# Convolution and max-pool on one core: the first quarter of the first pair loaded as fp32, identity and zeros set ahead of the casting loads, and all instructions in another order

## The chip, the cores and the metric

The kernel runs on one core of a Trainium2 chip. The metric is device time in microseconds (us), the median of several runs. A profile is of one execution; its span is the time from the first to the last instruction, and a little lies around it. The engines are PE (TensorE, matrix products; PEld is its weight load), DVE (VectorE), ACT (ScalarE), POOL (GpSimd) and SP (SyncE, which issues DMA transfers). ACT and POOL can issue transfers too; those of POOL can change the type on the way.

## The reference

Sixteen images of 64 channels and 64x64 points are convolved with a 3x3 kernel into 128 channels, with a border of zeros, and each 2x2 block of the result is reduced to its maximum.

```python
batch, c_in, h, w, c_out, k = 16, 64, 64, 64, 128, 3
x_pad = np.pad(x, ((0, 0), (0, 0), (1, 1), (1, 1)))
conv[b, co] += weight[co, ci, kh, kw] * x_pad[b, ci, kh:kh+h, kw:kw+w]      # over ci, kh, kw
output[b, c, i, j] = np.max(conv[b, c, 2*i:2*i+2, 2*j:2*j+2])
```

## The kernel before, in words

**Tiling.** Two images share the 128 partitions (64 channels each), so there are eight pairs, held as bf16 in `rows_x`. A pair is cut into four quarters of 16 rows. That gives 32 steps, numbered in the order of `SEQ`; `W01` is pair 0, quarter 1. In a step, each of the two images (lane 0 and 1) has two accumulators A and B of 128x512 fp32, one bank each of the eight banks of PSUM. A product with one lane uses 64 of PE's 128 rows, and the products of the two lanes run side by side.

**Two ways to make a step.** With g0, g1, g2 the weights of the three kernel rows and r(-1), r0, r1, r2 four input rows around a pair of output rows:

- Kind K (steps 0, 2, 6 and 7): A = (g2-g1) r1 + g0 r(-1) (products `PAa`, `PAb`), B = (g0-g1) r0 + g2 r2 (`PBa`, `PBb`), then B = max(A, B), then B += g1 (r0+r1) (`PR`). The weight blocks are called D2, G0, D0, G2, G1. D2 and D0 are differences; G0, G1 and G2 are plain copies of the weights.
- Kind W (all others): products with differences and sums of rows, `P2` (block GM, rows E = r0-r1), `P0` and `P3` (blocks G0, G2, rows V), `P1` (block GP, rows S = r0+r1). GM and GP need the sum g0+g2, `gsum`.

Each product has three taps, one matrix product per column shift of the kernel. For step 0 alone the products of kind K are cut into an upper half (`a`, pooled rows 0 to 3) and a lower half (`b`).

**What the engines do for a step.** DVE and POOL make the row sums and differences (tokens `KS`, `S`, `E`, `V`, and `S2`, `E2`, `V2` for two steps at once, line 219). ACT copies A out (`EV`, lines 401 and 403) and, in kind W, seeds B from A (`SE`, line 415). DVE takes the maximum of B and that copy (`MX`, line 427). At the end the columns are reduced: ACT copies the odd ones out (`OD`, line 431) and DVE takes the maximum (`CM`, line 448), or DVE reduces alone (`RM`, line 436). Then SP stores the result.

**The start.** SP loads the weights (`wraw`) and the first nine rows of the first pair as fp32 (`first`, line 184). POOL loads all other rows with a cast to bf16 (`load`, line 180); the ranges stand in `LOADS`, and the first three are issued before anything else (`EARLY = 3`). Then POOL makes the identity for the transposes, while DVE sets `zeros` and the border rows of `rows_x` to zero. PE multiplies ones by ones until the weights are there. DVE and ACT make the weight blocks in bf16 (tokens `c.`, lines 211, 212 and 219), PE transposes each (`T`, line 252, three products), and DVE or ACT copies it out of PSUM into `wt` (`TV`, lines 263 and 267). `XO` and `XE` cast the odd and the even rows of `first` into `rows_x`.

**What sets the order.** Nothing is scheduled by a compiler. `ORDER` is a list of tokens; each emits one instruction (a product token one tap) on the engine that it names, and each engine works through its own instructions in that order. An instruction waits for what it reads and for the buffer that it writes, and everything behind it on its engine waits too. Two rules beside it: a row operation on POOL is put behind the last one on DVE (`behind`), and a transfer takes one of eight semaphores in turn.

## Time and profile before

| | us |
|---|---|
| median of the runs (99.55 to 99.73) | 99.69 |
| the profiled execution | 99.57 |
| its span | 97.8 |
| PE busy (845 products) | 92.4 |
| DVE busy | 88.9 |
| ACT busy | 82.9 |
| POOL busy | 68.4 |
| first product of step 0 starts at | 5.55 |
| last load from HBM issued by POOL, time to landing (median of the 1 MB loads) | 13.5 |

Times in a timeline count from the span's start. A row of a timeline has the start, the time taken, the engine, the line, the operation, the tile written and read and the number of instructions merged; in brackets stands the idle time before it and what ended that. Instructions of an engine overlap a little, so two of 0.35 us in a row can take 0.62. A row of the DMA view has a queue, the packets, the megabytes and the share of the time of the 16 DMA engines; a row of an issue ends with the time from issue to landing. The granted clock of PE was 1.00 in nearly all of the span.

### The profile page before, as it was taken

To read this page: it belongs to the slowest core of one execution; us is meant where nothing else is said; L and a number is where in the kernel's file an instruction comes from. 1 tells how busy PE (TensorE), PEld (TensorE's weight loads), DVE (VectorE), ACT (ScalarE), POOL (GpSimd) and SP (SyncE) were. 2 spreads that over 40 slices of the span, in tenths; PEclk is the share of its full clock that TensorE was granted. 3 is DMA by queue.
4 is the path that set the end of the run, shared out by engine and by line. 5 is a ranking of instruction groups with operands and counts; after the bars stand their busy time and mean duration, and the time that the engine had idled before them with its cause. 6 is when DMAs were issued, how large, how long until landed. Compare 5 with 4: busy or idle time off the path is not lost.

```text
span 97.8 us, 2315 instructions
## 1 busy us (share of the span) xinstructions
PE 92.4 (94%) x845; PEld 57.6 (59%) x845; DVE 88.9 (91%) x172; ACT 82.9 (85%) x177; POOL 68.4 (70%) x60
## 2 busy tenths in 40 slices
PE   6998999999999999999999999999999999999920
PEld 2394554555886885666667555564555557777600
DVE  3459999999999999999999999999998999997960
ACT  5466688599779999999999999999989999889830
POOL 5994545936488867989584876759499779599200
PEclk9999999999999999999999999999999999999998
DMA  2999999999999999999999740405050503254052
GB/s 55 237 145 196 169 204 216 218 233 230 250 225 244 225 245 330 238 227 299 225 230 291 285 144 27 188 3 189 32 214 0 217 4 137 84 214 144 17 188 80
DMA packets 7675, 17.36 MB, mean 178 GB/s; under 512 B 624, under 2 KB 2544, under 8 KB 7024
## 3 DMA queue, kind: packets, MB, share of 16 engines
q0 software_dynamic: 2160, 8.24, 43.3%
q1 hardware_dynamic: 5216, 8.72, 25.6%
q10 hardware_dynamic: 288, 0.26, 0.8%
q8 instruction: 6, 0.10, 0.4%
q14 instruction: 5, 0.04, 0.1%
HBM read 17.07 MB, written 8.39 MB: 260 GB/s over the span
## 4 chain that ended last, share of the span: by engine, by line
PE 83%; POOL 5%; DVE 4%; issue 3%; ACT 1%; ACTq 0%; POOLq 0%
PE acc L369 82%; POOL rows_x L180 4%; DVE o L448 2%; DVE acc L427 1%; POOL gsum L219 1%; ACT acc L415 1%; PE acc L252 1%; DVE wq L219 1%; ACT ev L401 1%; POOL ident masks.py:199 0%; POOL ident masks.py:197 0%; ACTq L415 0%; POOLq L534 0%
## 5 line engine op out<-in xcount | busy, mean ns | idle before, releaser
L369 PEld LDWEIGHTS <-wt 64*128 64x128 bf16 x816 | 55.2, 94 | 31.2 <-issue 1.8
L369 PE MATMUL acc<-wv,wt 64*128 64x504 bf16 (+1 forms) x264 | 49.9, 377 | 0.0
L427 DVE TENSOR_TENSOR acc<-acc,ev 128x512 f32<-128x512 f32 x64 | 42.7, 689 | 1.2 <-ACT acc L415 0.5
L369 PE MATMUL acc<-ws,wt 64*128 64x512 bf16 (+1 forms) x168 | 40.8, 376 | 0.0
L369 PE MATMUL acc<-we,wt 64*128 64x512 bf16 (+1 forms) x168 | 39.3, 377 | 0.0
L401 ACT ACTIVATE ev<-acc 128x512 f32<-128x512 f32 x56 | 32.7, 605 | 1.8 <-PE acc L369 1.7
L415 ACT COPY acc<-acc 128x512 f32<-128x512 f32 x56 | 32.2, 590 | 2.1 <-PE acc L369 1.3
L219 POOL TENSOR_TENSOR ws<-rows_x 128x512 bf16<-128x512 bf16 (+1 forms) x12 | 17.6, 1477 | 4.2 <-DVE wv L219 1.9
L431 ACT COPY od<-acc 128x256 f32<-128x256 f32 x49 | 18.0, 379 | 2.8 <-PE acc L369 2.3
L219 POOL TENSOR_TENSOR we<-rows_x 128x512 bf16<-128x512 bf16 (+1 forms) x10 | 15.4, 1542 | 6.3 <-DVE wv L219 3.8
L448 DVE TENSOR_TENSOR o<-acc,od 128x256 f32<-128x256 f32 (+1 forms) x48 | 19.1, 420 | 0.1
L369 PE MATMUL acc<-rows_x,wt 64*128 64x504 bf16 (+7 forms) x120 | 16.5, 332 | 0.0
L219 POOL TENSOR_TENSOR wv<-rows_x 128x1024 bf16<-128x1024 bf16 (+1 forms) x6 | 14.7, 2449 | 2.3 <-DVE ws L219 1.6
L369 PE MATMUL acc<-vh,wt 64*128 64x504 bf16 (+1 forms) x72 | 16.0, 377 | 0.0
L219 POOL TENSOR_TENSOR vh<-rows_x 128x512 bf16<-128x512 bf16 x8 | 9.2, 1155 | 5.6 <-DVE we L219 3.1
L436 DVE TENSOR_REDUCE o<-acc 128x256 f32<-128x512 f32 x15 | 10.2, 680 | 0.0
L180 POOL DMA_DIRECT2D rows_x<-in_x_dram x15 | 8.6, 575 | 2.1 <-DMA rows_x<-in_x_dram 1.3
L219 DVE TENSOR_TENSOR wv<-rows_x 128x1024 bf16<-128x1024 bf16 (+1 forms) x11 | 9.8, 891 | 0.0
L369 PE MATMUL acc<-ks,wt 64*128 64x504 bf16 (+1 forms) x24 | 6.0, 376 | 0.0
L403 ACT COPY ev<-acc 128x512 f32<-128x512 f32 x8 | 4.5, 586 | 0.9 <-PE acc L369 0.9
L219 DVE TENSOR_TENSOR we<-rows_x 128x1024 bf16<-128x1024 bf16 (+1 forms) x9 | 5.1, 564 | 0.0
L219 DVE TENSOR_TENSOR ws<-rows_x 128x512 bf16<-128x512 bf16 (+1 forms) x8 | 4.7, 588 | 0.0
(26 smaller groups left out, 24.1 us busy)
## 6 DMA issues: line engine op xcount, KB each, us to landing
out_dram<-o SPq DMA_DIRECT2D x13, 512.0 KB, 6.5
rows_x<-in_x_dram POOLq DMA_DIRECT2D x5, 1024.0 KB, 13.5
rows_x<-in_x_dram POOLq DMA_DIRECT2D x4, 256.0 KB, 8.4
out_dram<-o SPq DMA_DIRECT2D x3, 256.0 KB, 2.9
rows_x<-in_x_dram POOLq DMA_DIRECT2D x1, 528.0 KB, 11.9
out_dram<-o SPq DMA_DIRECT2D x4, 128.0 KB, 2.0
rows_x<-in_x_dram POOLq DMA_DIRECT2D x1, 496.0 KB, 12.7
rows_x<-in_x_dram POOLq DMA_DIRECT2D x2, 240.0 KB, 9.1
```

Source lines behind the costliest of these rows:

```text
L180: nc.gpsimd.dma_start(out=xs[p][:, lo + 1 : hi + 1, :], in_=rows_of(p, lo, hi))
L219: inst = eng[e].tensor_tensor(out=out, in0=in0, in1=in1, op=op)
L252: nc.tensor.transpose(tp[:, (j - lo) * 128 : (j - lo + 1) * 128], wq[:, BLOCKS[m]].rearrange("a i j c -> a (i j c)")[:, (j - lo) * CI : (j ...
L369: yield lambda kw=kw, o0=o0, o1=o1, c0=c0, c1=c1: nc.tensor.matmul(acc[t][:, i0:i1, o0:o1], wt[l * CI : l * CI + CI, K * BLOCKS[block] + T ...
L401: nc.scalar.mul(t, acc[bank["A", s, l]], -1.0)
L403: nc.scalar.copy(out=t, in_=acc[bank["A", s, l]])
L415: nc.scalar.copy(out=acc[b], in_=acc[bank["A", s, l]])
L427: nc.vector.tensor_tensor(out=t, in0=t, in1=lanes(ev[s], l), op=MAX)
L431: nc.scalar.copy(out=t[:, l], in_=sums(s, l)[..., 1::2])
L436: nc.vector.tensor_reduce(out=lanes(outs(s), l), in_=pairs, axis=mybir.AxisListType.X, op=MAX,)
L448: nc.vector.tensor_tensor(out=t, in0=a[..., 0::2], in1=u, op=MAX)
```

## The change

Five things change.

1. The first transfer of `first` stays, and a second one loads rows 9 to 16 as fp32 as well, on SP. `LOADS` loses its first entry, so POOL's first casting load is rows 17 to 32. `XO` and `XE` come twice, for rows 0 to 8 and rows 9 to 16.
2. `EARLY` is 0: POOL makes the identity first, then `zeros` (DVE did that before), and the casting loads follow where `ORDER` has them.
3. `TAPS_FIRST = 1`: in step 0 the products with the plain blocks (`PBb` with G2, `PAb` with G0) come first and open their accumulators; those with the differences (`PAa`, `PBa`) add to them.
4. `ORDER` is another list throughout. Which row operations DVE and POOL do, which two steps they join, the banks and the place of every load but the sequence of the loads are set anew. One seed of B goes to DVE (`SEv`).
5. Two functions `sums_begin` and `sums_end` are defined for the tokens `SC` and `SA`. The new `ORDER` has no such token.

```diff
-LOADS = ((0, 9, 17), (0, 17, 33), (0, 33, 49), (0, 49, 64), (1, 0, 17), ...
-EARLY = 3
+LOADS = ((0, 17, 33), (0, 33, 49), (0, 49, 64), (1, 0, 17), ...
+EARLY = 0
+TAPS_FIRST = 1
 ORDER = """
-LH.3 LH.4 c.g0:a c.D2:v LH.5 c.g2:v c.g1:a T.D2:0 T.G0:1 LH.6 c.D0:v TV.D2:a T.G2:2 T.G1:3 TV.G0:a LH.7
+LH.0 LH.1 c.g2:v c.g0:a c.D2:v T.G2:0 c.g1:a T.G0:1 c.D0:v T.D2:2 XE.0a:a T.G1:3 TV.G2:v XO.0a:a T.D0:4
...
-    first = const.tile([128, R + 1, W], FP32, name="first")
-    nc.sync.dma_start(out=first, in_=rows_of(0, 0, R + 1))
+    first = const.tile([128, 2 * R + 1, W], FP32, name="first")
+    for lo, hi in ((0, R + 1), (R + 1, 2 * R + 1)):
+        nc.sync.dma_start(out=first[:, lo:hi], in_=rows_of(0, lo, hi))
     for k in range(EARLY):
         load(k)
     ident = const.tile([128, 128], BF16)
     make_identity(nc, ident)
     zeros = const.tile([128, 512], BF16)
-    nc.vector.memset(zeros, 0.0)
+    nc.gpsimd.memset(zeros, 0.0)
...
-    def to_bf16(odd, e):
-        cast(e, xs[0][:, 1 + odd : R + 2 : 2, :], first[:, odd : R + 1 : 2, :])
+    def to_bf16(odd, part, e):
+        lo, hi = (0, R + 1) if part == "a" else (R + 1, 2 * R + 1)
+        lo += (lo + odd) % 2
+        cast(e, xs[0][:, lo + 1 : hi + 1 : 2, :], first[:, lo:hi:2, :])
...
-            return block, i0, i1, rows, first and part != "b"
+            return block, i0, i1, rows, first != (TAPS_FIRST and s == 0) and part != "b"
```

How the new order moves instructions, at three places. First POOL, from the end of the common start-up on, before:

```order
L180 DMA rows_x<-in_x_dram 128x512
L180 DMA rows_x<-in_x_dram 128x1024 x2
masks.py:197 MEMSET ident 128x128
masks.py:199 ISA
masks.py:199 AFFINE_SELECT ident<-ident 128x128 [waits Pool_49]
L180 DMA rows_x<-in_x_dram 128x960
L180 DMA rows_x<-in_x_dram 128x1088
L180 DMA rows_x<-in_x_dram 128x1024 x2
L180 DMA rows_x<-in_x_dram 128x960
L219 TENSOR_TENSOR gsum<-wraw 128x192 [waits DMAHW0_49,DVE_49]
```

The same place of the changed kernel (its lines are a few higher: 182 is `load`, 224 the row operations):

```order
masks.py:197 MEMSET ident 128x128
masks.py:199 ISA
masks.py:199 AFFINE_SELECT ident<-ident 128x128 [waits Pool_49]
L193 MEMSET zeros 128x512
L182 DMA rows_x<-in_x_dram 128x1024 x2
L224 TENSOR_TENSOR gsum<-wraw 128x192 [waits DMAHW0_49,DVE_49]
L182 DMA rows_x<-in_x_dram 128x960
L182 DMA rows_x<-in_x_dram 128x1088
```

`gsum` now stands behind two loads instead of eight, and the loads of rows 17 to 32 and 33 to 48 (128x1024 each) behind identity and zeros. Second DVE, from the weights' arrival to the first row maxima, before:

```order
L219 TENSOR_TENSOR wq<-wraw 128x256 [waits DMAHW0_49]
L212 CAST wq<-wraw 128x256
L219 TENSOR_TENSOR wq<-wraw 128x256
L212 CAST rows_x<-first 128x4x64 [waits DMAHW1_49]
L267 COPY wt<-acc 128x384 [waits PE_49]
L267 COPY wt<-acc 128x384
L219 TENSOR_TENSOR wq<-gsum,wraw 128x256 [waits Pool_49]
L219 TENSOR_TENSOR ks<-rows_x 128x512 [waits DMASW0_49,DVE_49,Activation_49]
L267 COPY wt<-acc 128x384
L219 TENSOR_TENSOR wq<-gsum,wraw 128x256
L219 TENSOR_TENSOR we<-rows_x 128x512 [waits DMASW1_49]
L427 TENSOR_TENSOR acc<-acc,ev 128x512 [waits DVE_49,PE_49,Activation_49]
```

And in the changed kernel:

```order
L215 CAST wq<-wraw 128x256 [waits DMAHW0_49]
L224 TENSOR_TENSOR wq<-wraw 128x256 x2
L272 COPY wt<-acc 128x384 [waits PE_49] x3
L215 CAST rows_x<-first 128x4x64 [waits DMAHW2_49]
L224 TENSOR_TENSOR wq<-gsum,wraw 128x256 [waits Pool_49]
L224 TENSOR_TENSOR wq<-gsum,wraw 128x256
L224 TENSOR_TENSOR ks<-rows_x 128x512 [waits DVE_49,Activation_49]
L224 TENSOR_TENSOR we<-rows_x 128x512 [waits DMASW0_49]
L224 TENSOR_TENSOR wv<-rows_x 128x1024
L270 TENSOR_SCALAR wt<-acc 128x384 [waits PE_49]
L442 TENSOR_TENSOR acc<-acc,ev 128x512 [waits PE_49,Activation_49] x2
```

G2 (the cast of `wq`) comes ahead of D2 and D0, all three copies out of PSUM ahead of the row cast, and a difference of rows (`wv`, V.1) and a copy now stand between E.1 (`we`) and the first maxima. E.1 waits for POOL's first casting load (`DMASW0`), which was its second. Third PE, where step 1's products (`we`) end and step 2's begin, before:

```order
L369 MATMUL acc<-we,wt 128x8x63
L369 LDWEIGHTS wt
L369 MATMUL acc<-ks,wt 128x512 [waits DVE_49]
L369 LDWEIGHTS wt [waits DMASW2_49]
L369 MATMUL acc<-rows_x,wt 128x512 [waits Activation_49]
```

And in the changed kernel:

```order
L384 MATMUL acc<-we,wt 128x8x63
L384 LDWEIGHTS wt
L384 MATMUL acc<-rows_x,wt 128x4x63
L384 LDWEIGHTS wt
L384 MATMUL acc<-rows_x,wt 128x4x63
L384 LDWEIGHTS wt [waits DMASW1_49]
L384 MATMUL acc<-rows_x,wt 128x512 [waits DVE_49]
```

In both, PE comes to wait for the load of rows 33 to 48 (`DMASW2` before, `DMASW1` now) right behind step 1's first products; the last products of step 0 (128x4x63) now stand among these, and `PR` (`ks`) behind step 2's.

More of the change, by code (lines that the diff above doesn't have):

```diff
@@ new lines @@
+c.GM:v XE.0b:a PAa.0.0a PAa.0.1a PAb.0.0b PAb.0.1b PAb.0.0b PAb.0.1b LH.3 PAb.0.0b PAb.0.1b PAa.0.0b
+PAa.0.1b c.GP:v PAa.0.0b PAa.0.1b PAa.0.0b PAa.0.1b T.GM:4 LH.4 PBb.0.0b PBa.0.1a KS.0:v PBb.0.0b PBa.0.1a
+PBb.0.0b PBa.0.1a TV.GM:a T.GP:3 E.1:v LH.5 PBa.0.0a PBb.0.1b EV.0.1 PBa.0.0a PBb.0.1b V.1:v PBa.0.0a
+PBb.0.1b PBa.0.1b P2.1.0:4 LH.6 PBa.0.1b EV.0.0 P2.1.0 PBa.0.1b P2.1.1:2 TV.GP:v P2.1.0 P2.1.1 S.1:g
+PBa.0.0b MX.0.1 P2.1.1 PBa.0.0b SE.1.0:7 PBa.0.0b PAa.2.0:3 PAa.2.1:5 PAa.2.0 PAa.2.1 MX.0.0 SE.1.1:1
@@ L110 @@
+OD.30.1 CM.31.1 ST.30.0 OD.31.0 CM.30.1 ST.31.1:a CM.31.0 ST.30.1 ST.31.0:a
 """
@@ L306, in two_quarters, with sums_begin, sums_end @@
         row[name, s], row[name, place.index((p, q + 1))] = t[:, 0:half], t[:, half:]
+    def sums_begin(p, e):
+        eng[e].dma_start(out=xs[p - B // 2 + 2][:, 1:H], in_=xs[p][:, 1:H])
+    def sums_end(p, h):
+        lo, hi = 1 + h * H // 2, H // 2 + h * H // 2
+        t = xs[p - B // 2 + 2]
+        nc.gpsimd.dma_start(out=t[:, lo:hi], in_=xs[p][:, lo + 1 : hi + 1], accum_op=ADD)
+        for q in (2 * h, 2 * h + 1):
+            row["S", place.index((p, q))] = t[:, 2 * R * q + 1 : 2 * R * q + 2 * R : 2]
     def all_rows(s, e):
@@ L483 @@
         elif name in ("XO", "XE"):
-            to_bf16(int(name == "XO"), at)
+            to_bf16(int(name == "XO"), args[0][1:], at)
         elif name == "T":
@@ L496 @@
             two_quarters(int(args[0]), name[0], at)
+        elif name == "SC":
+            sums_begin(int(args[0]), at)
+        elif name == "SA":
+            sums_end(int(args[0]), int(args[1]))
         elif name == "V":
```

183 lines of the change are left out of this document (89 added, 94 removed).

## The prediction

> **What bounds the kernel now.** I read the page's chain of waits first, then busy time by stage, then the first ten microseconds engine by engine. The profiled execution took 99.57 us, of which 97.8 us are its span and 1.8 us lie around it; the median of the runs shown is 99.69, so 0.12 us above the profiled one.
>
> ```profile
> PE 92.4 (94%) x845; PEld 57.6 (59%) x845; DVE 88.9 (91%) x172; ACT 82.9 (85%) x177; POOL 68.4 (70%) x60
> PE 83%; POOL 5%; DVE 4%; issue 3%; ACT 1%; ACTq 0%; POOLq 0%
> 3.75:5.55 1.80, 1.73 (x17) 1.03 (x15) 1.68 (x4) 1.79 (x4) 1.80 (x4) 1.00 0.88 124
> 5.55:7.66 2.11, 2.11 (x38) 1.70 (x36) 1.04 (x3) 1.24 (x4) 2.11 (x4) 1.00 1.05 167
> 7.66:9.38 1.72, 1.44 (x20) 0.91 (x19) 1.72 (x6) 0.95 (x2) 0.42 (x2) 1.00 1.12 206
> 9.38:89.10 79.72, 79.72 (x735) 50.39 (x736) 79.18 (x150) 73.33 (x158) 59.38 (x43) 1.00 0.73 186
> 89.10:97.80 8.70, 4.44 (x37) 2.56 (x34) 4.53 (x10) 4.36 (x10) 2.08 (x2) 0.95 0.35 117
> ```
>
> The last five rows are stretches: length, then busy time of PE, PEld, DVE, ACT and POOL, the clock, the share of the DMA engines and GB/s. From 9.38 to 89.1 us PE is never idle, and DVE has 79.72 - 79.18 = 0.54 us free: two engines are full, and what is done there can hardly be done sooner. The change does not alter the number of products, so a gain must come from the stretch before 9.38, where PE has holes. These are PE's and the weight loader's rows there:
>
> ```profile
> 4.42 1.20 PE L252 MATMUL acc<-ident,wq 128*128 128x128 bf16 x15
> 5.55 2.11 PE L369 MATMUL acc<-rows_x,wt 64*128 64x256 bf16 x36
> 7.92 0.17 PEld L252 LDWEIGHTS <-wq 128*128 128x128 bf16 x3 [0.53 <-DVE wq L219]
> 8.19 0.55 PEld L369 LDWEIGHTS <-wt 64*128 64x128 bf16 x12
> 9.04 0.17 PEld L252 LDWEIGHTS <-wq 128*128 128x128 bf16 x3 [0.30 <-DVE wq L219]
> 9.38 0.82 PE L369 MATMUL acc<-we,wt 64*128 64x512 bf16 x6
> 10.02 0.38 PE L369 MATMUL acc<-rows_x,wt 64*128 64x512 bf16 x1
> ```
>
> All 48 half-size products of step 0 lie between 5.55 and 9.04, and the loader stands idle 0.53 and 0.30 us before the two late transposes (GM and GP). Why those are late, the chain shows:
>
> ```profile
> 4.77 1.60 POOL rows_x L180 x3
> 6.37 0.85 POOL gsum L219
> 7.24 0.63 DVE wq L219
> 7.92 0.34 PE acc L252 x3
> ```
>
> POOL issues three more loads before it makes gsum; only then can DVE make GM, and PE transpose it.
>
> **The holes, added up.** Of the loader's 0.83 us not all is lost, since it runs ahead of the multiplications. The 36 products end at 7.66 by the modelled end, so the hole before 7.92 is between 0.25 and 0.53; I take 0.4. Before the second transposes it is between 0 (the twelve products end at 8.19 + 0.83 = 9.02) and 0.30; I take 0.2. Together 0.6, between 0.25 and 0.83. That is the most that the head can give, since nothing makes the first product much earlier:
>
> ```profile
> 3.75 0.61 DVE L219 TENSOR_TENSOR wq<-wraw 128x256 bf16<-128x256 f32 x1 [2.07 <-DMA wraw<-in_weight_dram]
> 4.28 0.38 DVE L212 CAST wq<-wraw 128x256 bf16<-128x256 f32 x1
> 4.58 0.62 DVE L219 TENSOR_TENSOR wq<-wraw 128x256 bf16<-128x256 f32 x1
> 5.66 0.62 DVE L267 COPY wt<-acc 128x384 bf16<-128x384 bf16 x2 [0.23 <-PE acc L252]
> 7.24 0.62 DVE L219 TENSOR_TENSOR wq<-gsum,wraw 128x256 bf16<-128x256 f32 x1 [0.96 <-POOL gsum L219]
> 7.78 0.42 DVE L219 TENSOR_TENSOR ks<-rows_x 128x512 bf16<-128x512 bf16 x1
> 3.75 1.20 ACT L211 CAST wq<-wraw 128x256 bf16<-128x256 f32 x2 [1.73 <-DMA wraw<-in_weight_dram]
> 5.70 0.47 ACT L211 CAST rows_x<-first 128x320 bf16<-128x320 f32 x1
> ```
>
> *Plain blocks first.* The same three DVE operations (G2, D2, D0) stand before T.D0 in another order; they end at 4.58 + 0.62 = 5.20 as before, and T.D0 still stands ahead of the first product. The new first product needs G2 copied out (DVE, 0.35 after 5.20) and the even rows (ACT, 3.75 + 1.20 + 0.47 = 5.42). First product again at about 5.55: worth nothing.
>
> *gsum earlier.* POOL now issues two loads before gsum, not eight. gsum can start when the weights are there, 3.75, and ends near 3.75 + 0.85 = 4.60 instead of 7.21. DVE, which sat idle 0.96 us for it, goes on: three copies out of PSUM (0.27 each from 5.11, since the pair took 0.62), the cast of the second odd rows, then GM from about 6.2 to 6.8, GP to 7.3 and the sum KS.0 to 7.6. PE reaches T.GM after 30 half products, so at 5.55 + 30/36 x 2.11 = 7.3: no hole. T.GP follows 0.6 later, after a transpose and six half products: none. This is the 0.6.
>
> *The second fp32 transfer.* It is a third transfer on SP, 256 KB, and brings two more casts to ACT (up to 0.47 each); DVE keeps one, now of the second part. ACT is busy for 1.24 of 2.11 us in that stretch, and behind these casts stand only copies that are used after 7 us. Cost nothing here; without ACT's idle 0.87 it would be up to 0.9, since the lower half of step 0 waits for the last of them.
>
> *Identity and zeros ahead of the casting loads.* Here the gain can be lost. The landings:
>
> ```profile
> 2.97 0.23 POOL masks.py:197 MEMSET ident<- 128x128 bf16 x1
> 1.19 0.48 DVE L191 MEMSET rows_x<- 128x512 uint32 x1
> rows_x<-in_x_dram POOLq DMA_DIRECT2D x1, 128.0 KB, 4.9
> rows_x<-in_x_dram POOLq DMA_DIRECT2D x1, 256.0 KB, 6.8
> rows_x<-in_x_dram POOLq DMA_DIRECT2D x1, 256.0 KB, 7.5
> q1 hardware_dynamic: 229, 0.48, 86.0%
> q0 software_dynamic: 91, 0.09, 63.6%
> q0 software_dynamic: 108, 0.15, 92.7%
> q0 software_dynamic: 192, 0.36, 101.9%
> ```
>
> The three loads (rows 9 to 16, 17 to 32, 33 to 48) were issued on POOL at 1.24, 1.93 and 2.46 and landed that much later: 6.1, 8.7 and 10.0. The four queue rows are the windows 1.7 to 3.5, 3.5 to 4.5, 4.5 to 6 and 6 to 8 us: POOL's queue moves nothing before 3.5, 2.3 us after its first issue, and then 0.09, 0.15 and 0.36 MB; SP's queue moves 0.48 MB in 1.8 us. In the changed kernel rows 17 to 32 are POOL's first load. It starts behind the identity (0.55 from its start to what follows) and the zeros. No trace shows zeros on POOL: at least the 0.27 us that DVE took for half as many elements, at most four times the identity's 0.23, so 0.92; I take 0.5, by DVE's 0.48 for 512 elements. With POOL free between 0.86 (DVE's first work) and 1.24, the issue falls between 1.7 and 2.7, about 2.1; the first packet at 4.4. In its old place this load landed 8.7 - 6.1 = 2.6 us after the one ahead of it; so it lands at 7.0, plus up to 1.0 us for the 0.26 MB that SP's third transfer shares the engines with (0.48 MB per 1.8 us): 7.0 to 8.0. Rows 33 to 48 land 1.3 us later, 8.3 to 9.3. If the engines are simply full from 2 us on, both land as before, 8.7 and 10.0.
>
> What is needed: DVE makes E.1 from rows 17 to 32, then V.1, GP's copy and MX.0.1, and PE's next product on step 0 stands behind MX.0.1; DVE is ready for E.1 at about 7.6. With PE 0.6 early this load must be there by 8.7 - 0.6 = 8.1, and rows 33 to 48, which PE itself waits for right after step 1's products (10.02 before, landing at 10.0), by 10.0 - 0.6 = 9.4. The estimates 7.0 to 8.0 and 8.3 to 9.3 just meet both; the upper bound misses both by 0.6. I take 0.1 us off for it: **0.5 us gained** at 10 us.
>
> *The new order of all else.* The counts of operations by engine, before and after, priced by these rows:
>
> ```profile
> L427 DVE TENSOR_TENSOR acc<-acc,ev 128x512 f32<-128x512 f32 x64 | 42.7, 689 | 1.2 <-ACT acc L415 0.5 <-ACT ev L401 0.2 <-PE acc L369 0.2
> L448 DVE TENSOR_TENSOR o<-acc,od 128x256 f32<-128x256 f32 x47 | 18.4, 414 | 0.1
> L436 DVE TENSOR_REDUCE o<-acc 128x256 f32<-128x512 f32 x15 | 10.2, 680 | 0.0
> L448 DVE TENSOR_TENSOR o<-acc,od 128x512 f32<-128x512 f32 x1 | 0.7, 687 | 0.0
> ```
>
> The row operations are the same in sum (62 units of 512 elements on DVE, 54 on POOL, before and after). DVE gets one copy between accumulators (0.69, as its 128x512 row) and one scaled copy out of PSUM (0.35) and loses a reduction (0.68). Final maxima are 50 instead of 49 units of 256, but three pairs are merged instead of one: 0.41 - 2 x 0.14 = 0.13. Four row maxima are merged into two, saving about 0.14 each. Sum +0.2 us; DVE has 0.96 more in the head, so it stays within its time. The tail is the same sequence but for S.30 and S.31 in one POOL operation. I add 0 for the middle, between -0.5 (DVE's idle 0.54 gone) and +1.0 (rival 3).
>
> A rule speaks against the change. The Trainium skill, "DMA: Bandwidth & Descriptors", section "Issuing engines are not separate DMA queues", says that transfers from SP, ACT and POOL all run on the same 16 engines and interleave, and that another issuer saves only issue time. By that rule the move of rows 9 to 16 to SP brings nothing forward; it is the rival "landings as before" below, and the windows' shares of 0.88 to 1.12 bear it out in part.
>
> **Rivals.**
> 1. *Landings as before.* The engines are full from 2 us, the bytes read ahead of rows 33 to 48 are the same, so they land at 10.0 and PE, early at 9.4, waits there. For it: shares of 0.88, 1.05 and 1.12 in the first three stretches. Against: 0.15 MB in 92.7% of 1.5 us is a slow start of POOL's queue, which SP's queue did not have. Time: 10.02 + 0 against 10.02, so 99.7, no change.
> 2. *First load too late: slower.* POOL starts at 1.24, zeros cost 0.92, the issue falls at 2.7 and the first packet at 5.0; loads one and two then need what they needed behind the first packet before, 10.0 - 3.5 = 6.5, less 0.7 for the smaller first one: rows 33 to 48 at 10.8. PE waits in order, so everything moves by 0.8: 99.69 + 0.75 = 100.4. It decides as soon as that load lands after 10.0. Against: it adds up all upper bounds.
> 3. *The order costs PE holes in the middle: slower.* With DVE busy 79.18 of 79.72 us, an operation that stands too early on it holds back a maximum, and with it the accumulator that PE's next step needs. A hole of half a maximum (0.35) at every tenth of the 31 later steps is three holes, 1.0 us, against 0.5 gained: 99.2 + 1.0 = 100.2. It decides above 0.5 us of new holes. For it: 0.54 us is a small reserve. Against: the counts are equal, and DVE enters the stretch earlier.
>
> **How the numbers follow.** Forecast 99.69 - 0.5 = 99.2, its own range 98.9 to 99.6; chance 0.50. Rival 1 0.18, rival 2 0.12, rival 3 0.20. A measurement tells 0.2% (0.2 us) from none. The forecast lies faster in all but 0.03; rival 1 lies within; rival 3 with under 0.7 us of holes counts 0.04 within. So faster 0.47, same 0.25, slower 0.28. The range leaves out a tenth at each end: 98.8 (0.83 of holes all gained) to 100.4.
>
> **What would show it.** Right: gsum on POOL before 5 us, no idle before the transposes of GM and GP, first product near 5.55, the first product on rows 33 to 48 near 9.5, PE full from there to about 88.6. Wrong: PE or its loader idle for a load around 9 us (rivals 1 and 2, told apart by the landing, 10.0 or later); PE busy below the stretch's length between 10 and 85 us, released by DVE or ACT (rival 3).

## The result, and the profile after

The changed kernel took 101.05 us (median of four runs, 100.33 to 101.96) beside 99.65 us (99.55 to 99.73) of the kernel before in the same session: a ratio of 1.0115, 95% interval 1.0088 to 1.0143. It is slower by 1.4 us where 0.5 us less was forecast, and lies outside the range of 98.8 to 100.4. Ratios leave out runs that lie over 1.5% above the fastest of the same kernel.

The profiled execution took 101.04 us, its span is 99.3 us. Here are the lines of its page on busy time and on the chain of waits, and then its stretches (length, busy time of PE, PEld, DVE, ACT and POOL with counts, clock, DMA share, GB/s).

```profile
PE 92.8 (93%) x845; PEld 55.6 (56%) x845; DVE 89.1 (90%) x169; ACT 82.8 (83%) x178; POOL 68.3 (69%) x61
...
PE 59%; DMA 26%; DVE 5%; ACT 2%; POOL 2%; issue 2%; SPq 1%; POOLq 0%; ACTq 0%
```

```profile
5.47:7.36 1.89, 1.08 (x20) 0.83 (x19) 0.81 (x4) 1.19 (x4) 1.89 (x4) 1.00 1.08 197
7.36:9.45 2.09, 2.09 (x32) 1.41 (x32) 2.09 (x5) 1.00 (x4) 1.31 (x3) 1.00 0.97 130
9.45:29.00 19.55, 19.55 (x189) 10.65 (x185) 19.04 (x34) 15.98 (x36) 12.56 (x12) 1.00 1.03 201
29.00:34.50 5.50, 4.93 (x45) 2.97 (x43) 4.50 (x10) 3.68 (x10) 3.45 (x3) 1.00 1.04 238
34.50:89.10 54.60, 54.60 (x504) 34.92 (x502) 53.86 (x104) 52.29 (x113) 43.93 (x31) 1.00 0.59 175
```

The busy times hardly differ from those of before, so no work was added. The chain did change: it had no DMA to speak of and now has 26%. PE is full from 9.45 to 29.0 and again from 34.5 to 89.1; there are two places where it is not. PE's rows in the first:

```profile
5.47 1.08 PE L384 MATMUL acc<-rows_x,wt 64*128 64x256 bf16 x18
7.36 0.83 PE L384 MATMUL acc<-rows_x,wt 64*128 64x256 bf16 x12 [0.81 <-DVE rows_x L215]
...
8.40 0.50 PE L384 MATMUL acc<-rows_x,wt 64*128 64x256 bf16 x6
...
9.11 0.50 PE L384 MATMUL acc<-rows_x,wt 64*128 64x256 bf16 x6
9.45 0.38 PE L384 MATMUL acc<-we,wt 64*128 64x512 bf16 x1
```

The first product is at 5.47 as forecast. Then PE waits 0.81 us for DVE's cast of rows 9 to 16, and comes to step 1 at 9.45 with 18 + 12 + 6 + 6 = 42 of the 48 half-size products done; before, it came there at 9.38 with all 48. Six of them take 2.11 / 36 x 6 = 0.35 us, so the head is 0.07 + 0.35 = 0.42 us later, where 0.5 less was forecast. The second place is in the same trace's timeline of DVE and of PE around 30 us:

```profile
28.76 0.42 DVE L224 TENSOR_TENSOR we<-rows_x 128x512 bf16<-128x512 bf16 x1
30.18 0.43 DVE L224 TENSOR_TENSOR vh<-rows_x 128x512 bf16<-128x512 bf16 x1 [1.00 <-DMA rows_x<-in_x_dram]
30.52 0.69 DVE L442 TENSOR_TENSOR acc<-acc,ev 128x512 f32<-128x512 f32 x1
```

```profile
30.35 0.38 PE L384 MATMUL acc<-ws,wt 64*128 64x504 bf16 x1
31.27 0.37 PE L384 MATMUL acc<-ks,wt 64*128 64x512 bf16 x1 [0.54 <-DVE acc L442]
```

PE is released by a maximum on DVE (L442), which by itself would look like rival 3 of the prediction. But DVE was late only because `vh`, one place ahead of it, had waited 1.00 us for a load: that of pair 3. Counted in products, by the window from 30 to 35 us, first of the kernel before, then of the changed one:

```profile
30.00:35.00 5.00, 5.00 (x49) 3.71 (x47) 5.00 (x11) 4.73 (x12) 4.63 (x4) 1.00 1.03 233
30.00:35.00 5.00, 4.43 (x40) 2.34 (x38) 4.82 (x10) 3.36 (x9) 3.95 (x4) 1.00 1.03 237
```

Instead of 49 products PE does 40, and nine products at 5.00 / 49 = 0.10 us are some 0.9 us. The end of PE's work shows the sum: its last row starts at 92.96 and lasts 2.02 us, in the kernel before 92.39 and 1.15 us, so 1.44 us later, against 101.04 - 99.57 = 1.47 us between the two profiled executions. The head gives 0.42 of it, the stretch around 30 us most of the other 1.0.

The chain in order of time tells why both transfers are late (start, time taken, what):

```profile
1.65 5.34 DMA first<-in_x_dram
...
7.58 8.73 DMA rows_x<-in_x_dram
...
16.48 0.85 POOL ks L224
...
17.60 1.10 POOL we L224
18.70 11.46 DMA rows_x<-in_x_dram
...
30.18 0.04 DVE vh L224
```

The second fp32 transfer takes 5.34 us from its issue, the first one took 3.3. The load of pair 3 is issued at 18.70, behind two row operations on POOL, the first of which waits for another load; before, it was issued at 10.62. POOL's rows of the changed kernel:

```profile
1.72 1.23 POOL L182 DMA_DIRECT2D rows_x<-in_x_dram  x2
5.22 0.82 POOL L224 TENSOR_TENSOR gsum<-wraw 128x192 f32<-128x192 f32 x1 [2.27 <-DVE wq L224]
5.98 2.69 POOL L182 DMA_DIRECT2D rows_x<-in_x_dram  x5
...
13.43 1.16 POOL L224 TENSOR_TENSOR ws<-rows_x 128x512 bf16<-128x512 bf16 x1 [2.50 <-DVE wv L224]
14.53 1.10 POOL L182 DMA_DIRECT2D rows_x<-in_x_dram  x2
...
18.70 0.58 POOL L182 DMA_DIRECT2D rows_x<-in_x_dram  x1
```

Issuing stops from 2.95 to 5.98, because `gsum` waits for the last of DVE's weight operations (the rule `behind`) and five loads stand behind it, and again from 8.7 to 14.5, because `S.1` and `S.3` stand ahead and wait, `S.3` for DVE. So the queue of casting loads moves less in two places. Its rows from 8 to 12 and from 14 to 18 us, first of the kernel before, then of the changed one (packets, MB, share of the 16 engines' time):

```profile
q0 software_dynamic: 399, 0.72, 109.7%
q0 software_dynamic: 304, 0.85, 109.2%
```

```profile
q0 software_dynamic: 293, 0.54, 100.0%
q0 software_dynamic: 242, 0.58, 90.6%
```

From 8 to 12 us a quarter of the megabytes is missing, though the packets' time still fills the engines; from 14 to 18 us both fall.

### The profile page after: what moved, and what is told of

Its sections match the earlier page's. It is cut to its first block, busy times and chain, and to the rows that moved or that the text cites. A ratio compares the mean times of both kernels' runs of the same rounds, so it can differ in the third digit from the quotient of the medians.

```text
span 99.3 us, 2327 instructions
## 1 busy us (share of the span) xinstructions
PE 92.8 (93%) x845; PEld 55.6 (56%) x845; DVE 89.1 (90%) x169; ACT 82.8 (83%) x178; POOL 68.3 (69%) x61
## 3 DMA queue, kind: packets, MB, share of 16 engines
q0 software_dynamic: 2016, 8.11, 43.1%
## 4 chain that ended last, share of the span: by engine, by line
PE 59%; DMA 26%; DVE 5%; ACT 2%; POOL 2%; issue 2%; SPq 1%; POOLq 0%; ACTq 0%
PE acc L384 59%; DMA rows_x<-in_x_dram 20%; DMA first<-in_x_dram 5%; DVE acc L442 2%; DVE o L463 2%; ACT acc L430 1%; POOL we L224 1%; ACT ev L416 1%; POOL ks L224 1%; SPq L187 0%; SPq L184 0%; DVE rows_x L215 0%; DVE wq L224 0%; POOLq L224 0%; DVE vh L224 0%
## 5 line engine op out<-in xcount | busy, mean ns | idle before, releaser
L384 PE MATMUL acc<-wv,wt 64*128 64x504 bf16 (+1 forms) x276 | 56.7, 377 | 0.0
L442 DVE TENSOR_TENSOR acc<-acc,ev 128x512 f32<-128x512 f32 (+1 forms) x62 | 42.6, 709 | 0.8 <-PE acc L384 0.2
L384 PE MATMUL acc<-we,wt 64*128 64x512 bf16 (+1 forms) x168 | 41.3, 377 | 0.0
L224 POOL TENSOR_TENSOR ws<-rows_x 128x512 bf16<-128x512 bf16 (+1 forms) x12 | 19.6, 1639 | 11.9 <-DVE wv L224 4.2
L224 POOL TENSOR_TENSOR we<-rows_x 128x512 bf16<-128x512 bf16 (+1 forms) x12 | 17.7, 1476 | 4.1 <-DVE vh L224 1.9
L384 PE MATMUL acc<-rows_x,wt 64*128 64x504 bf16 (+6 forms) x120 | 17.0, 332 | 0.8 <-DVE rows_x L215 0.8
L384 PE MATMUL acc<-vh,wt 64*128 64x504 bf16 (+1 forms) x60 | 13.3, 376 | 0.0
L224 POOL TENSOR_TENSOR wv<-rows_x 128x1024 bf16<-128x1024 bf16 x5 | 10.7, 2131 | 2.9 <-DVE wv L224 1.5
L224 DVE TENSOR_TENSOR we<-rows_x 128x512 bf16<-128x512 bf16 (+1 forms) x10 | 4.7, 477 | 0.0
L481 PE MATMUL acc<-const-bfloat16-1.0 128*128 128x512 bf16 x8 | 3.6, 625 | 0.8 <-PEq L553 0.8
```

The source lines that it names most:

```text
L224: inst = eng[e].tensor_tensor(out=out, in0=in0, in1=in1, op=op)
L384: yield lambda kw=kw, o0=o0, o1=o1, c0=c0, c1=c1: nc.tensor.matmul(acc[t][:, i0:i1, o0:o1], wt[l * CI : l * CI + CI, K * BLOCKS[block] + T ...
L442: nc.vector.tensor_tensor(out=t, in0=t, in1=lanes(ev[s], l), op=MAX)
L481: nc.tensor.matmul(acc[n], ones[:, 0:128], ones, start=True, stop=True, skip_group_check=True)
```

## The experiments

The theories. For the middle, M1: the loads of pairs 2 and 3 are issued too late on POOL, and the queue runs dry; M2: the engines were busy all along, so issue times do not matter; M3: the order on DVE and ACT. For the head, H1: the second fp32 transfer is held up beside the first casting loads, and PE waits for it; rivals are named where they come up. Issue and landing of the loads that matter, in us, from the semaphore records of the traces:

| | before | after | a_loads_early_2 | a_gsum_behind | b_combo |
|---|---|---|---|---|---|
| second fp32 transfer | - | 1.65, 6.99 | 1.65, 7.44 | 1.64, 7.16 | 1.65, 7.05 |
| rows 17 to 32 | 1.93, 8.69 | 1.72, 7.34 | 1.72, 7.86 | 1.72, 8.21 | 1.72, 8.35 |
| rows 33 to 48 | 2.46, 9.97 | 2.42, 8.64 | 2.41, 9.14 | 2.41, 9.47 | 2.41, 9.59 |
| rows 49 to 63 | 3.52, 11.12 | 5.98, 11.39 | 6.02, 10.81 | 2.94, 10.66 | 2.94, 10.78 |
| pair 1, last part | 5.81, 16.48 | 8.11, 17.29 | 8.14, 16.84 | 5.01, 16.17 | 5.12, 16.55 |
| pair 2, first half | 7.11, 19.01 | 14.53, 20.41 | 8.66, 19.36 | 14.69, 20.22 | 6.41, 19.08 |
| pair 3 | 10.62, 27.30 | 18.70, 30.16 | 11.34, 28.15 | 18.81, 30.54 | 10.95, 27.33 |

**a_loads_early and a_loads_early_2** (one kernel, run twice).

```diff
-... LH.6 ... S.1:g ... S.3:g ... LH.7 ... LH.8 ... E.5:g ... LH.9 ...
+... LH.6 LH.7 LH.8 ... S.1:g LH.9 ... S.3:g ... E.5:g ...
```

> The changed kernel, with three loads issued earlier on POOL and nothing else moved: the two of pair 2 right behind the last of pair 1, the one of pair 3 right behind the row sum S.1. Theory M1 (the loads of pairs 2 and 3 are issued too late, at 14.5, 15.1 and 18.7 us, behind row operations that wait for other loads, so that DMA runs dry): pair 3 lands near 27 to 28 us instead of 30.16, the PE holes of 0.8 us at 30.25 and 0.4 at 33.64 go, and the time falls by 1.0 to 1.2 us, ratio to the kernel before near 1.000. Rival M2 (DMA was busy all along with the added fp32 bytes, so issue times do not matter): pair 3 still lands near 30, no change, ratio near 1.0115. Rival M3 (the holes come from the order of operations on DVE and ACT, the load being only the last of several): the landing moves but holes of over 0.5 us stay near 30 to 34.

> The kernel a_loads_early once more, for a trace of an ordinary run (the first trace is of a run 1.5 us over the others). Theory M1: pair 3 lands at 28 to 29.5 us, no hole over 0.4 us at 30 to 34, and what is left over b_combo lies before 16 us, where rows 49 to 63 and pair 1 come late (issued behind gsum, at 6.0 us and after): a hole of about 0.5 to 1 us between 9 and 16 us. Rival: pair 3 lands near 30 and the hole at 30 us stays.

Measured: 100.45 us (six runs, 100.11 to 101.95), ratio 1.0083, interval 1.0052 to 1.0115; the second time 100.79 us (two runs), 1.0124, 1.0088 to 1.0160. In the second trace pair 3 lands at 28.15, and DVE goes through the place without a wait:

```profile
29.23 0.42 DVE L222 TENSOR_TENSOR we<-rows_x 128x512 bf16<-128x512 bf16 x1
29.56 0.42 DVE L222 TENSOR_TENSOR vh<-rows_x 128x512 bf16<-128x512 bf16 x1
```

In this trace the hole at 30 us is gone with nothing but three issues moved; M2 and M3 fall for it. The times alone do not show a gain: both intervals overlap that of the changed kernel (1.0088 to 1.0143). The expected hole before 16 us is not in this trace. The first trace, of the run of 101.95, has one: rows 49 to 63 land at 13.35, DVE waits 2.05 us for them and PE 1.25 us behind it; pair 3 lands at 31.09 there. It shows no more than that such runs occur. What is left of the loss in the second trace is the head: the first product is at 5.88 instead of 5.47, and PE waits 0.55 us for rows 9 to 16. Part of that is not the order. These are PE's fifteen transposes ahead of the first product, here and then in the trace of b_combo, an experiment below:

```profile
4.17 1.78 PE L255 MATMUL acc<-ident,wq 128*128 128x128 bf16 x15
```

```profile
4.15 1.27 PE L255 MATMUL acc<-ident,wq 128*128 128x128 bf16 x15
```

The traces record PE's clock at full speed from 6.57 us on here and from 4.24 us on there; from 5 to 6 us PE does 11 products here and 20 there. (The clock column of the stretches shows 1.00 ahead of the first record too.) So the half microsecond between the two first products (5.88 and 5.36) goes with the clock and not with the loads.

**a_pair3_early.** `LH.9` alone is moved, right behind `LH.8`.

> The changed kernel, with only the load of pair 3 moved: right behind the second load of pair 2 (issued near 15.2 instead of 18.7 us). It tells which of the dry stretches of DMA counts. If the wait between the issue of pair 2 and that of pair 3 counts (15.1 to 18.7), pair 3 lands 1.5 to 2.5 us earlier than 30.16 and the holes near 30 shrink to under 0.3 us, ratio near 1.003. If the late issue of pair 2 (14.5) is the larger part, it lands about 0.5 to 1 us earlier, half of the hole stays, ratio near 1.007. If issue times do not matter (M2), no change, 1.0115.

Measured: 100.96 us (four runs), ratio 1.0119, 1.0086 to 1.0151. Issued at 16.35 instead of 18.70, pair 3 lands at 30.64. No gain, and the first outcome falls. By itself that would also fit M2; beside a_loads_early_2, where pair 2 is moved as well and the hole is gone, it says that the gap ahead of pair 2 (issued at 15.3 here) counts.

**a_gsum_behind.** `LH.2` to `LH.6` ahead of `c.GS:g`.

> The changed kernel, with gsum moved back behind seven loads on POOL (two before it in the changed kernel, eight in the kernel before); POOL, which waits from 3.0 to 5.2 us for the DVE operation that gsum stands behind, issues five loads in that time. If that wait starves DMA (theory M1 for the first 14 us): the loads of rows 49 to 63 and of pair 1 land 1.0 to 1.5 us earlier than 11.39, 13.60, 14.86, 16.31 and 17.29, gsum starts only about 0.3 us later (near 5.5), and the time falls by 0 to 0.4 us (ratio 1.007 to 1.0115), since the loads of pairs 2 and 3 stand behind row operations that these loads release. If DMA is full in any case (M2): landings as in the changed kernel, time the same or 0.1 to 0.3 us longer for the later gsum.

Measured: 101.13 us (four runs), ratio 1.0143, 1.0112 to 1.0174. The loads of rows 49 to 63 and of pair 1 land 0.7 to 1.3 us earlier, as M1 says (those of rows 17 to 48 0.8 to 0.9 us later), but pair 3 is issued at 18.81 and lands at 30.54: the queue only moves still less from 14 to 18 us, 0.51 MB. The gain of 0 to 0.4 us did not come.

**b_combo.** Both together.

```diff
-LH.0 LH.1 ... c.GS:g ... LH.2 ... LH.6 ... S.1:g ... LH.7 ... LH.8 ... LH.9
+LH.0 LH.1 LH.2 LH.3 LH.4 LH.5 LH.6 ... c.GS:g LH.7 LH.8 ... S.1:g LH.9
```

> The changed kernel with all its loads up to pair 3 issued about as early as in the kernel before: seven casting loads ahead of gsum, the two of pair 2 right behind it, that of pair 3 right behind the row sum S.1; all else as changed. Each half of this alone left a hole near 30 us, because the queue ran dry at another place (near 9 us in the one, near 15 to 18 us in the other). Theory M1 (only the two together keep the queue of casting loads full): no dry place from 6 to 24 us, pair 3 lands at 27.0 to 28.5 us, no PE hole over 0.3 us from 28 to 34; what is left against the kernel before is the head (0.4 to 1.0 us later, by when the second fp32 transfer lands): ratio 1.003 to 1.008. Rival M3 (order of DVE and ACT): holes of over 0.5 us in sum stay at 30 to 34 though pair 3 is there, ratio 1.010 or more.

Measured: 99.65 us (twelve runs, 99.20 to 100.77), ratio 0.9985, 0.9943 to 1.0027: the whole loss of the change is gone, 1.3% by the ratios, more than the 0.35 to 0.85% that was expected to come back, and the rest of the order is as changed. The same two windows of the queue, 8 to 12 and 14 to 18 us, and PE in 30 to 35:

```profile
q0 software_dynamic: 403, 0.73, 110.3%
q0 software_dynamic: 299, 0.85, 108.9%
```

```profile
30.00:35.00 5.00, 5.00 (x50) 3.64 (x47) 5.00 (x11) 4.34 (x11) 4.64 (x5) 1.00 1.05 233
```

The queue is as full as before, and 50 products run where the changed kernel had 40: M1 is shown for the middle, by the times and by the trace. The head of this trace still has its wait:

```profile
7.42 0.83 PE L382 MATMUL acc<-rows_x,wt 64*128 64x256 bf16 x12 [0.98 <-DVE rows_x L213]
```

PE's work ends 0.4 us later than in the kernel before, all of it from the head. The trace is of a run of 99.97 us, 0.3 above the median; what the head costs in the faster runs no trace shows.

**a_cast_late** (a measurement). `LH.0` and `LH.1` stand behind `c.GS:g`.

> A measurement, not a better version: the changed kernel, with its first two casting loads moved behind gsum, so that POOL's queue starts at about 6 us and not at 1.7. Theory H1 (the second fp32 transfer, which lands at 6.99 and makes the PE hole of 1.0 us at 6.28, is held up by the casting loads that start beside it at 4.4): it lands at 5.3 or before, and the hole at 6.28 is gone. Rival H2 (a third transfer on SP's queue takes that long by itself): it lands at 6 to 7 as before. In both the rows 17 to 48 come some 3 to 4 us later, so PE waits near 9 us and the time grows by 2 to 4 us, ratio 1.03 to 1.05.

Measured: 103.27 us (two runs), ratio 1.0366. With no load of POOL beside it the second fp32 transfer lands 3.6 us after its issue, at 5.27, and PE runs 30 products without a stop:

```profile
first<-in_x_dram SPq DMA_DIRECT2D x1, 256.0 KB, 3.6
```

```profile
5.88 1.75 PE L382 MATMUL acc<-rows_x,wt 64*128 64x256 bf16 x30
```

(The time is lost at 10.8 us, where PE waits 1.63 us for the late rows 17 to 32, and again around 30 us as in the changed kernel.) Beside casting loads that are issued at 1.72 it landed at 5.36, 6.54, 6.99, 7.05, 7.16, 7.44, 7.71 and 7.74 in eight traces, of the changed kernel and its relatives. So H2 falls, and H1 is borne out by seven of the eight and by one trace without those loads; the 5.36 says that they do not always hold it up. What is left of the transfer late is little; in the changed kernel, the rows of SP's queue in the windows 5 to 6 and 6 to 7.2 us:

```profile
q1 hardware_dynamic: 13, 0.02, 9.6%
q1 hardware_dynamic: 5, 0.01, 1.7%
```

Eighteen of over a hundred packets, 0.03 of 0.26 MB. Of the 16 counts that make up the landing, 12 had come by 4.91; the last four came at 5.27, 6.10, 6.77 and 6.99. PE waits for the slowest.

**c_before_fp32 and c_before_fp32_2.** The kernel before with the second fp32 transfer alone.

```diff
-EARLY = 3
+EARLY = 2
-    nc.sync.dma_start(out=first, in_=rows_of(0, 0, R + 1))
+    for lo, hi in ((0, R + 1), (R + 1, 2 * R + 1)):
+        nc.sync.dma_start(out=first[:, lo:hi], in_=rows_of(0, lo, hi))
-... TV.G2:v PAa.0.0b ...
+... TV.G2:v XO.0b:v XE.0b:a PAa.0.0b ...
```

> The kernel before with one part of the change alone: rows 9 to 16 come as fp32 by a second transfer on SP, with one cast on DVE and one on ACT behind the copies of D0 and G2; POOL issues the two loads of rows 17 to 48 at 1.24 and 1.8 us, then the identity. By the prediction (cost nothing, loads earlier): rows 17 to 32 land at 7.0 to 8.0, rows 33 to 48 at 8.3 to 9.3, no hole near 6.3, the holes before GM and GP stay, ratio 0.995 to 1.000. By theory H1 (the fp32 transfer and the start of the casting loads hold each other up): the fp32 transfer lands at 5.3 to 7.7 and not in the same place twice, PE has a hole of 0 to 1.5 us before the lower half of step 0, ratio 1.000 to 1.012.

> c_before_fp32 once more, since its six runs lay between 100.6 and 103.9 us: is that the kernel or the occasion? If the second fp32 transfer beside the first casting loads makes the head of the kernel before a lottery (its landing decides a PE hole at 6.3 us of 0.7 to some us): again a wide spread, 100.3 to 103, ratio 1.01 to 1.03. If the occasion was disturbed: 99.9 to 100.6, ratio 1.003 to 1.010, as the trace's last product (0.6 us later than before) says.

Measured: 100.59 to 103.88 us (six runs), ratio 1.0126, 1.0025 to 1.0228, which rests on two of the six; the second time 102.36 to 105.71 (four runs, no ratio). This part alone makes the kernel before slower: its fastest run of ten is 1.05 us above the median of the kernel before. How much slower is not settled. The wide spread came again, so it is the kernel. In the first trace, of the fastest run, the transfer lands at 6.70, and other loads up to 2.3 us sooner than before (rows 33 to 48 of pair 0 at 8.24 against 9.97), which buys nothing. In the second one of its 16 counts comes at 8.71, 2.0 us behind the fifteenth, and PE stands for it:

```profile
5.60 0.75 PE L382 MATMUL acc<-rows_x,wt 64*128 64x256 bf16 x12
9.08 2.75 PE L382 MATMUL acc<-rows_x,wt 64*128 64x256 bf16 x24 [2.72 <-DVE rows_x L213]
```

The transfer is not alone in that: the last count of POOL's first load, rows 17 to 32, comes at 8.52, 2.2 us behind its fifteenth.

**b_combo_cast9.** b_combo with rows 9 to 16 by a casting load again, POOL's first, at 1.72 us.

> The same as b_combo, but rows 9 to 16 come by a casting load again (POOL's first, behind identity and zeros), and the second fp32 transfer with its two casts is gone. It undoes the fp32 part alone. Theory H3 (the fp32 transfer is what opens the hole near 6.3 us, since it shares the engines with the start of the casting loads): rows 9 to 16 land near 6.1 plus 0.5 = 6.6 us, later loads 0.5 us later than in the kernel before, the hole near 6.3 shrinks by 0 to 0.4 us and one of about 0.5 us opens before the products on rows 33 to 48 (landing 10.5): the time is within 0.4 us of b_combo on either side. Rival H4 (without the fp32 transfer the head of the changed kernel would be faster than that of the kernel before): 0.5 us or more below b_combo, ratio below 1.000.

Measured: 100.05 us (twelve runs), ratio 1.0032, 0.9994 to 1.0069. Rows 9 to 16 land at 7.72, later than the 6.6 expected, and PE waits as in b_combo. H4 falls: the transfer is not the only thing that makes these rows late; a first casting load that is issued at 1.72 was no sooner here (it was in c_before_ident below, at 6.84).

**c_before_ident.** The kernel before with `EARLY = 0`, identity and zeros on POOL, then `LH.0 LH.1 LH.2`.

> The kernel before with one part of the change alone: the identity first on POOL, then the zeros (on POOL instead of DVE), then the first three casting loads, which are issued at 1.72, 2.2 and 2.9 us instead of 1.24, 1.93 and 2.46. If the head of the kernel before hangs on these loads (rows 33 to 48 land at 10.0 just as PE comes to them): each lands 0.4 to 0.5 us later, PE waits near 10 us, the time grows by 0.3 to 0.6 us, ratio 1.003 to 1.006. If the engines are full in any case from 2 to 8 us (rival 1 of the prediction): landings and time as before, 1.000.

Measured: 99.66 us (ten runs), ratio 1.0015, 0.9996 to 1.0034. Rows 9 to 16 land at 6.84 instead of 6.13 and PE waits 0.73 us for them, but rows 33 to 48 land at 9.40, not later than before, and the waits at GM are gone. The cost is 0.1 us, which the interval does not tell from none; neither outcome is right.

**c_before_gsum.** In the kernel before `c.GS:g` stands ahead of `c.D2:v`.

> The kernel before with gsum alone moved: ahead of the DVE operations on the weights, so that it starts on POOL near 4.0 us instead of 6.37; loads behind it start 0.85 us later. By the prediction's term (0.6 us of holes before GM and GP go): GM near 6.2 us, both holes gone, and the gain is kept only as far as loads allow. If rows 17 to 32 (8.7) and 33 to 48 (10.0) land as before, PE waits for them and the gain is 0.0 to 0.1 us: ratio 0.999 to 1.000. If gsum earlier is worth its 0.6 by itself: ratio 0.994.

Measured: 100.02 us (twelve runs), ratio 1.0025, 0.9994 to 1.0055. Neither: `gsum` starts at 4.61, but the cast on DVE that overlaps it takes four times as long as in the kernel before (0.38 us), and the first product comes at 6.55 instead of 5.55:

```profile
4.09 1.59 DVE L211 CAST wq<-wraw 128x256 bf16<-128x256 f32 x1
```

```profile
4.61 0.81 POOL L218 TENSOR_TENSOR gsum<-wraw 128x192 f32<-128x192 f32 x1
```

Still, only about half of that 1.0 us reaches the end (PE's work ends 0.47 us later than in the kernel before, and the medians are 100.02 and 99.54): the holes at the transposes are gone.

**d_gm_first and e_upper_first** try to fill the wait of b_combo's head. The first edit below is d_gm_first against b_combo, the second e_upper_first against d_gm_first.

```diff
-... LH.6 ... c.GS:g ... XO.0b:v ... c.GM:v ... PAb.0.0b ... c.GP:v ... T.GM:4 PBb.0.0b ... T.GP:3 ...
+... c.GS:g LH.6 ... c.GM:v XO.0b:v ... T.GM:4 PAb.0.0b ... c.GP:v ... T.GP:3 PBb.0.0b ...
```

```diff
-... PAa.0.0a PAa.0.1a T.GM:4 PAb.0.0b ... PBb.0.0b PBa.0.1a ...
+... PAa.0.0a PAa.0.1a PBa.0.0a PBa.0.1a ... T.GM:4 PAb.0.0b ... PBb.0.0b PBb.0.1b ...
```

> b_combo with the head's order mended round the late fp32 transfer: on DVE GM ahead of the cast of the odd rows 9 to 16, on PE the transposes of GM ahead of the lower half of step 0 and those of GP six products sooner, and gsum behind six casting loads instead of seven (so that it starts by 5.3 us). In b_combo PE waited at 6.16 for 1.15 us for the casts of the second fp32 transfer (landing 7.05) and did the transposes of GM (0.35 us) after that. Theory H1 (the wait for that transfer is the cost of the head): the transposes of GM fall into the wait, the gain is 0.35 us, at most 0.7 if the casts come earlier too: ratio 0.993 to 0.996. Rival: the head does not decide, since the load of rows 33 to 48 (9.6 us) ends last there anyway: no change from b_combo, 0.9985.

> d_gm_first with the rest of step 0's upper half (six products with D0 on rows 0 to 8, PBa) ahead of the transposes of GM and of the lower half, so that PE has 0.35 us more work before it needs rows 9 to 16. With a first product at 5.5, PE then comes to the lower half near 7.0 us. Theory H1 (in the head PE waits for the second fp32 transfer alone, at 6.5 to 7.7 us): 0.2 to 0.5 us less than d_gm_first, ratio 0.995 to 0.999. Rival H5 (the loads of rows 17 to 48, at 8.3 and 9.6, end last whatever stands before them, so every gain ahead of them is given back): the hole moves to 9 or 10 us, the same as d_gm_first, 1.0018.

Measured: 99.55 us, ratio 1.0018, 0.9994 to 1.0042; and 99.77 us, 1.0010, 0.9991 to 1.0030 (twelve runs each). The gains expected are not there. In the trace of d_gm_first the transfer lands at 6.54, early for it, and PE does not wait for it. In the trace of e_upper_first the transfer lands at 7.71 and PE waits for it all the same, now with 24 products and the transposes of GM done:

```profile
8.08 0.83 PE L382 MATMUL acc<-rows_x,wt 64*128 64x256 bf16 x12 [0.82 <-DVE rows_x L213]
```

**e_start_before and f_best.** e_upper_first with the start of the kernel before (`EARLY = 3`, one fp32 transfer, zeros on DVE); then with `LH.6` behind `c.GS:g`.

> e_upper_first with the start of the kernel before: three casting loads at 1.24 us, first of all on POOL, rows 9 to 16 among them, then the identity; zeros on DVE; no second fp32 transfer. It undoes parts 1 and 2 of the change and keeps the new order. Theory H6 (the start of the change is the loss of its head, its order the gain): rows 9 to 16 land near 6.1, rows 33 to 48 near 9.5 to 10.0, no hole near 6.3 and none at the transposes, ratio 0.994 to 0.998, below e_upper_first. If the loads cap it (H5): PE waits near 9.5 to 10 us and the ratio is 0.998 to 1.001. If identity behind three loads (at 3.0 us) delays the first transposes: first product at 5.6 or later, ratio 1.000 or more.

> e_start_before with gsum one load sooner on POOL (behind six loads instead of seven), so that it starts at 5.2 instead of 5.78 us. In e_start_before PE stood 0.45 us for GM at 7.33 and came to step 1 at 8.98, with rows 17 to 32 there at 8.2. Theory (GM, and so gsum, ends last in that head, and the loads have room): GM is ready at 6.65, the wait goes, step 1 starts near 8.6 us just behind the load of rows 17 to 32, and the time falls by 0.3 to 0.4 us: ratio 0.996 to 0.998, faster than the kernel before. Rival H5 (the loads cap it): the wait moves to rows 17 to 32 or 33 to 48, the same as e_start_before, 1.0008.

Measured: 99.62 us, ratio 1.0008, 0.9994 to 1.0023; and 99.50 us (99.04 to 99.98), 0.9993, 0.9974 to 1.0012 (twelve runs each). In e_start_before PE waited 0.45 us for GM; in f_best that wait is gone and another one stands in its place, for rows 17 to 32 (landing 8.87 in this trace):

```profile
8.90 0.42 DVE L221 TENSOR_TENSOR we<-rows_x 128x512 bf16<-128x512 bf16 x1 [1.26 <-DMA rows_x<-in_x_dram]
```

```profile
9.38 0.37 PE L381 MATMUL acc<-we,wt 64*128 64x512 bf16 x1 [0.32 <-DVE we L221]
```

In f_best's trace H5 holds: what PE gains ahead of rows 17 to 32 it gives back at their landing, and that landing moves by up to 1 us from trace to trace of these four kernels (7.93 to 8.87). That it is what caps the other three is not shown: PE's wait there is for the fp32 transfer (e_upper_first), for GM (e_start_before) or too short to name (d_gm_first). No version is faster than the kernel before by more than the measurement tells.

## Why the prediction was wrong, step by step

- *What bounds the kernel, and that a gain must come from the head*: right. DVE and PE are as full as before, and outside the two places named no stretch lost more than some 0.15 us.
- *Plain blocks first, worth nothing*: right; 5.47 against "about 5.55".
- *Identity and zeros ahead of the casting loads*: right in the changed kernel's trace, and that trace was lucky. Rows 17 to 32 were put at 7.0 to 8.0 and landed at 7.34, rows 33 to 48 at 8.3 to 9.3 and landed at 8.64. The zeros took 0.53 us on POOL (0.5 taken), the issue came at 1.72 instead of 2.1. In the seven other traces that issue these two loads at the same times they landed at 7.86 to 8.69 and at 9.14 to 9.97; one of them (a_pair3_early) has them where the kernel before has them, as rival 1 said. Rival 2, with 10.8, falls in all eight. By the rule of the Trainium skill, "DMA: Bandwidth & Descriptors", section "Issuing engines are not separate DMA queues", that was weighed there, another issuer saves only issue time; in the changed kernel's trace the two loads came 1.3 us sooner, but rows 9 to 16, moved to SP, came 0.9 us later (6.99 against 6.13), so for the rows that were moved the rule was on the right side.
- *gsum earlier* ("can start when the weights are there, 3.75"): mis-sized. It started at 5.22, since `behind` puts it after DVE's last weight operation; the prediction had described that rule and did not apply it. It was still early enough for GM. What the step left out is the queue behind it: five loads wait with `gsum` for 3 us. In f_best's trace the wait for GM is gone and a wait for a load stands in its place, so there the 0.6 us were not kept.
- *The second fp32 transfer* ("Cost nothing here"): this step failed. It counted the bytes against the loads behind them and asked when ACT and DVE would do the casts, but not when the transfer itself lands. The runs put that at 6.5 to 7.7 us in most traces, beside the starting casting loads, and at 5.27 without them; PE waits 0.81 us. With c_before_fp32 the part alone costs 1 us or more; in the new order a casting load in its place (b_combo_cast9) was no better, so what it costs there against another way to bring these rows is open.
- *The new order of all else* ("I add 0 for the middle"): this step failed by the larger sum, 1.0 us. It priced every operation of DVE and no issue on POOL, though the place of every load was part of the change. Rival 3 had the place (PE released by DVE) and about the price (1.0), but not the mechanism: b_combo keeps the order of DVE, ACT and PE, moves eight issues beside `gsum`, and has no hole there. With the loads early, +0.2 us of DVE work and the rest of the order cost nothing that shows.
- *The range* took one such loss at a time; two came, 0.42 + 1.0 us, and 99.57 + 1.44 = 101.0. With the loads early, b_combo is at 99.65, 0.45 us above the forecast of 99.2.

What stays open: how the 0.8 us between a_loads_early and b_combo (100.45 and 99.65) divide, and which of the two transfers yields to the other at the start, run by run. A difference of half a microsecond between the heads of two single traces is not a finding: the first product lies between 5.36 and 5.96 in kernels that are nearly alike up to there (c_before_gsum aside), and most of that goes with the clock. In the six traces whose records have the clock at full speed only from 5.44 us or later, the first product comes at 5.78 to 5.93; in the others at 5.36 to 5.60, but for d_gm_first, where the first rows landed only at 5.43.

## What to carry to other kernels

When an order is changed, list for each queue the time of every issue and what the issuing engine waits for just ahead of it: a load that stands behind an operation that itself waits for a load leaves the DMA engines short of work, and the bill came 12 us later here, under the name of another engine. Look at all such places together: closing the first alone (a_gsum_behind) only lengthened the second. A small transfer on the path is as late as the slowest of its 16 parts; beside a starting stream of large loads it came 1.3 to 2.5 us later than without in seven traces of eight, so do not count it as free.

## What the runs showed of the hardware

- *A cast on DVE was four times as long beside `gsum` on POOL.* The 128x256 cast from fp32 took 0.38 us in the kernel before and 1.59 in c_before_gsum, where `gsum` falls into it. That POOL holds it up is argued, not shown: the edit moved `gsum` alone, but the cast starts 0.52 us ahead of it and in 0.38 us would have been over, and three copies out of PSUM beside `gsum` in the changed kernel took 0.89 us as elsewhere. The Trainium skill, "GPSIMD Engine Reference", section "Key points", says that GpSimd shares its SBUF interfaces with VectorE and that this contends with some of its instructions; this one cast fits that.
- *Few of the 16 parts of a transfer lag.* One to four counts came up to 2.2 us behind the rest (c_before_fp32_2, the changed kernel, a_loads_early_2). "DMA: Bandwidth & Descriptors" in the Trainium skill, section "Latency and other measured facts", says that two of the engines are usually slower, with POOL's kind of transfer as its guess at the cause. The traces agree that it is a few, and beside POOL's loads; they do not show which.
- *The clock falls within a wait of 2.7 us.* In c_before_fp32_2 PE stands from 6.35 to 9.08 us. The granted clock (the third value from the right) is at half for some 3.4 us, and PE's 24 products behind the wait took 2.75 us, where 24 took 1.41 in e_upper_first:

```profile
8.00:9.00 1.00, 0.00 (x0) 0.00 (x0) 0.27 (x2) 0.27 (x1) 0.20 (x1) 0.67 1.10 205
9.00:10.00 1.00, 0.92 (x10) 0.77 (x11) 1.00 (x4) 0.13 (x1) 0.34 (x1) 0.50 1.15 211
10.00:11.00 1.00, 1.00 (x14) 0.81 (x12) 1.00 (x3) 0.42 (x1) 0.00 (x0) 0.50 1.10 202
11.00:12.00 1.00, 1.00 (x11) 0.47 (x7) 0.01 (x1) 0.65 (x2) 0.84 (x1) 0.62 1.10 203
```

By the averages 0.67 and 0.62 of the first and the last row it lasts from 8.3 to 11.8 us, so it starts 2.0 us into the wait. That is 1.3 us more on top of the wait of 2.72, and may be a part of why that kernel's times spread so far; the wait of 0.81 us in the changed kernel left the clock at 1.00. The Trainium skill, "TensorE: Matmul & The Clock Gate", section "What's actually happening", says that the clock goes to half after an idle window of about 3.4 us and back after a busy one; the trace agrees on the half and on the 3.4 us that it lasts, while the wait that set it off was shorter. The records of the clock in the 17 traces show how that goes together. In each trace the changes of the clock lie whole multiples of 3.41 us apart (3.41 and 3.42 us in c_before_fp32_2, 88.7 to 95.6 us from the rise to the fall at the end, 26 to 28 times 3.41). Take PE's busy share in the stretches of 3.41 us between such points: the clock fell after stretches with 44% or less (42% in c_before_fp32_2, from 4.93 to 8.35 us), stayed full after 55% or more, rose after 79% or more and stayed at half after 70% or less. So it is the place of a wait in that grid that counts, beside its length: the 1.51 us that PE waits in the head of a_pair3_early left 56% of its stretch busy, and the clock stayed full.
